# Two blocks of a transformer on one core: the modulation products of conv_ffn's out stage move into fox attention and the even mixer

## The chip, the cores and the metric

The kernel runs on one core of a Trainium2 chip. Five engines work beside each other, each through its own list of instructions: TensorE (PE, matrix products), VectorE (DVE), ScalarE (ACT), GpSimd (POOL) and SyncE (SP), which here issues nearly all DMA transfers. The metric is the device time of one execution in microseconds (us). Three runs of the kernel before took 1831.75, 1835.52 and 1836.30 us; their median is 1835.52.

## The reference

All matrices are f32, d = 1024, 256 positions (272 with 16 `meta` positions in the first block). The first block is a recurrent mixer, `conv_ffn`, forgetting attention ("fox") and `conv_ffn` again, with layer norms; the second has two layers of `swiglu`, a mixer (even: latent plus sparse attention; odd: dilated plus block attention) and `swiglu`. Every part of the second block is modulated by columns that depend on the input `c` alone:

```python
def conv_ffn(x, w_in, conv_w, conv_b, w_out):
    h = causal_dwconv(x @ w_in, conv_w, conv_b)
    gate, val = h[..., :D_FF], h[..., D_FF:]
    return (jax.nn.gelu(gate) * val) @ w_out

def modulate(x, g, shift, scale):
    return rms_norm(x, g) * (1.0 + scale[:, None, :]) + shift[:, None, :]

def swiglu(y, w_in, w_out):
    a, b = jnp.split(y @ w_in, 2, axis=-1)
    return (jax.nn.silu(a) * b) @ w_out
```

Shift, scale and gate of the six modulated parts are `silu(c) @ ada_w + ada_b`, for each layer a vector of 9216 numbers out of a 1024 x 9216 matrix. They need nothing of the activations, so their products may be computed at any time before their part begins.

## The kernel before, in words

Activations lie transposed, channels on the 128 partitions and positions along the row. Each f32 product is three matmuls (`mm3`, lines 54 to 56) of operands split into a high and a low part: ACT casts the high part of a weight block `raw` to `wh` (line 47), DVE subtracts it to get `wl` (line 50, POOL in a few places). Weights come by 1 MB DMAs that SP issues in the order of the program into five buffers `raw`; `wh` and `wl` have five buffers each as well. A DMA waits on SP for its buffer, and whatever SP issues afterwards waits behind it.

The stages follow each other: recurrent mixer, conv_ffn(0) to about 390 us, fox to about 550, conv_ffn(1) to about 770, swiglu(0,0) to about 967, even mixer to about 1115, swiglu(0,1) and swiglu(1,0) to about 1510, odd mixer to about 1635, swiglu(1,1).

*The modulation* (`ada`, line 859 and after) is cut into 72 units. A unit brings one megabyte of `ada_w` into a `raw` buffer (line 869), beside the weights, and multiplies its four blocks of 128 x 512 by a column of `silu(c)` each and adds them up on DVE: line 878 opens a sum, line 880 adds to it, so an even unit is one of 878 and three of 880, an odd unit four of 880. After every second unit the sum's columns are formed: four small matmuls (line 890) over the partitions, a copy on ACT (line 894), a transpose on PE (line 896), an addition on DVE (line 899). `ada_late` puts these some units behind. `self.plan` says in which step of which stage a unit stands: "conv" for the steps of conv_ffn's first product, "out" for the steps of the second product (`gemm_out`), for conv_ffn and swiglu alike, "swiglu" for the steps of swiglu's first product. `scales`, which needs the columns of a part, issues what is still missing.

*conv_ffn's first product* goes in steps of 128 channels: PE fills a PSUM tile `pg`, ACT (584) and DVE (586) add up the three shifted copies, ACT (607) and POOL (608) form gate times value, ACT (47) and POOL (50) split it. *Fox* begins with projections: ACT and DVE compute the forget gates' sums (lines 690 to 718, `atanh_series` at 547 to 551), PE transposes the values, DVE copies them to `V` and `vM` (lines 645, 646), and PE's line 654 multiplies `vM`, ahead of the scores (798 to 802). Its attention is run by `pipeline`, which calls `fill` between the jobs. *Modulated parts* begin with sums of squares on PE (966), POOL (992), a reciprocal root on DVE (341 to 343) and the product with x (973, 976, 980, 983).

The order on each engine is made by a scheduler: it simulates the program with costs of its own and puts instructions that need nothing of each other in another order than they are written in. Products of `ada`, which need only their weights, are often pulled ahead by it.

Of the kernel before, what the change touches and what calls it, by code (L numbers as in the profile page):

```python
# [26 lines left out]
class Kernel:  # L27
# [93 lines left out]
    def gemm_out(self, W, K, xs, epilogue, load=None, mid=None, before=None, pool=False):  # L121
# [3 lines left out]
        for half in range(2):  # L125
# [3 lines left out]
            for k0, kn in groups:  # L129
# [28 lines left out]
                if not last and k0:  # L158
                    self.ada(int(K > 2000 and (half, k0) in self.plan["out"]))
# [465 lines left out]
    def fox(self):  # L625
# [50 lines left out]
        for g in range(2):  # L676
# [55 lines left out]
            if g == 0:  # L732
                steps = (
                    self.gemm_steps(W, [(512, 512)], self.xh, self.xl, 0, L, k_epi),
                    self.gemm_steps(Wq, [(512, 512)], self.xh, self.xl, 14, L, q_epi),
                )
                self.pipeline(jobs, lambda i: 0 <= i < 8 and next(steps[i // 4], None))
# [3 lines left out]
        def fill(i):  # L741
            if i >= 0:
                next(first, None)
                next(sg, None)
            if i > 2:
                gate(3 + i // 2)
# [112 lines left out]
    def ada(self, n):  # L859
# [4 lines left out]
        for _ in range(min(n, 72 - self.ada_i)):  # L864
# [7 lines left out]
            if k0 == 0:  # L872
                self.ada_sum = self.tile([128, 512], "p")
# [11 lines left out]
    def ada_sums(self, l, b, s):  # L885

        nc = self.nc
        ps = self.psum("s")
        for j in range(4):
            nc.tensor.matmul(  # L890
                ps[32 * j : 32 * j + 32, 0:128], self.onesD[:, 0:32], s[:, j * 128 : j * 128 + 128], start=True, stop=True
            )
        e = self.tile([128, 128], "e")
        nc.scalar.activation(e, ps[:, 0:128], AF.Copy, scale=float(D))

        def columns():
            ps = self.psum("s")
            self.transpose(ps[:, 0:128], e)
            nc.vector.tensor_add(
                self.mod[l][:, 4 * b : 4 * b + 4],  # L900
                ps[:, 0:128].rearrange("p (j r) -> p j r", r=32)[:, :, 0],
                self.col_ada[l][:, 4 * b : 4 * b + 4],
            )

        self.late.append((self.ada_i + 1, 18 * l + b, columns))
# [104 lines left out]
    def swiglu(self, l, f):  # L1010
# [49 lines left out]
        for c0 in range(0, DF2, 256):  # L1060
# [40 lines left out]
            self.ada(int(c0 // 256 in self.plan["swiglu"]))  # L1101
# [123 lines left out]
    def even_mixer(self, l):  # L1225
# [23 lines left out]
        for cs in ((1440, 280), (928, 512)):  # L1249
            for _ in steps(*cs):  # L1250
                if i == 4:
# [32 lines left out]
        def fill(i):  # L1284
# [9 lines left out]
            if i > 2:  # L1294
                next(side, None)

# [695 lines left out]
    def run(self, upto=99):  # L1992
        tc, a = self.tc, self.a
        with (
# [5 lines left out]
            bufs = {"raw": 5, "wh": 5, "wl": 5, "e": 9, "p": 5, "pt": 3, "st": 8, "G": 4, "ns": 7, "st0": 1, "st1": 4, "st4": 3, "st5": 3}  # L2000
            pb = {"g": 4, "s": 4}

            def tile_(shape, tag, dt=F32, bufs_=None, **kw):
# [9 lines left out]
                "swiglu": range(9),  # L2013
# [124 lines left out]
```

## Time and profile before

| | |
|---|---|
| median of three runs | 1835.52 us |
| the profiled execution | 1832.26 us |
| its span | 1830.5 us |
| PE busy, share of the span | 1771.1 us, 97% |
| DVE busy | 1390.4 us, 76% |
| ACT busy | 1013.3 us, 55% |
| POOL busy | 427.3 us, 23% |
| HBM read | 358.21 MB, 196 GB/s |

The profile is of one execution. PE's busy time includes matmuls at half clock, so a stretch at half clock costs time without an idle row. A row of a timeline gives start, duration, engine, line, operation, tiles, how many instructions are merged in it, and in brackets how long the engine idled ahead of it and what released it.

### The profile page before, as it was taken

To read this page: it belongs to the slowest core of one execution; us is meant where nothing else is said; L and a number is where in the kernel's file an instruction comes from. 1 tells how busy PE (TensorE), PEld (TensorE's weight loads), DVE (VectorE), ACT (ScalarE), POOL (GpSimd) and SP (SyncE) were. 2 spreads that over 40 slices of the span, in tenths; PEclk is the share of its full clock that TensorE was granted. 3 is DMA by queue.
4 is the path that set the end of the run, shared out by engine and by line. 5 is a ranking of instruction groups with operands and counts; after the bars stand their busy time and mean duration, and the time that the engine had idled before them with its cause. 6 is when DMAs were issued, how large, how long until landed. Compare 5 with 4: busy or idle time off the path is not lost.

```text
span 1830.5 us, 34951 instructions
## 1 busy us (share of the span) xinstructions
PE 1771.1 (97%) x13819; PEld 1672.7 (91%) x13819; DVE 1390.4 (76%) x2500; ACT 1013.3 (55%) x1803; POOL 427.3 (23%) x430
## 2 busy tenths in 40 slices
PE   9999999999998999989999899999999999999999
PEld 8998999998888989889998659999999999889998
DVE  7989987887679787898666868877786668866543
ACT  6965765465557554454436656544454436565442
POOL 0025332230245332432101302211022110013210
PEclk9999999999999999999999999999999999999999
DMA  7553667744344767569774704988597874536550
GB/s 210 154 185 114 221 224 242 247 151 143 113 133 149 241 210 253 185 209 322 248 243 159 197 13 157 335 268 295 194 297 244 286 249 139 173 93 201 177 199 30
DMA packets 290564, 361.55 MB, mean 198 GB/s; under 512 B 12464, under 2 KB 208687, under 8 KB 290400
## 3 DMA queue, kind: packets, MB, share of 16 engines
q1 hardware_dynamic: 290096, 359.14, 60.3%
q8 instruction: 109, 1.79, 0.4%
q14 instruction: 55, 0.45, 0.1%
q10 hardware_dynamic: 304, 0.18, 0.0%
HBM read 358.21 MB, written 1.08 MB: 196 GB/s over the span
## 4 chain that ended last, share of the span: by engine, by line
PE 77%; DVE 10%; ACT 3%; issue 2%; POOL 1%; DMA 0%; DVEq 0%; POOLq 0%; ACTq 0%
PE pg L54 22%; PE pg L56 21%; PE pg L55 21%; DVE wl L50 2%; PE pg L1129 2%; PE pg L1127 2%; PE pg L1128 2%; PE ps L186 1%; PE ps L1199 1%; DVE e L586 1%; DVE B L311 1%; ACT wh L47 1%; PE ps L890 1%; DVE p L880 0%; POOL e L608 0%
## 5 line engine op out<-in xcount | busy, mean ns | idle before, releaser
L47 ACT CAST wh<-raw 128x1024 fp32r<-128x1024 f32 (+5 forms) x553 | 547.3, 998 | 515.3 <-PE pg L55 364.7
L50 DVE TENSOR_TENSOR wl<-raw,wh 128x1024 fp32r<-128x1024 f32 (+5 forms) x547 | 644.4, 1185 | 233.9 <-ACT wh L47 232.0
L54 PE MATMUL pg<-B,wh 128*128 128x256 f32 (+4 forms) x2136 | 622.2, 292 | 6.1 <-DVE e L586 4.1
L56 PE MATMUL pg<-B,wl 128*128 128x256 f32 (+4 forms) x2136 | 608.9, 285 | 2.2 <-DVE wl L50 2.2
L55 PE MATMUL pg<-B,wh 128*128 128x256 f32 (+5 forms) x2104 | 598.3, 284 | 4.3 <-POOL B L983 2.5
L55 PE MATMUL pg<-xl,wh 128*128 128x256 f32 (+4 forms) x1688 | 480.3, 285 | 0.5 <-POOL xl L983 0.5
L54 PE MATMUL pg<-xh,wh 128*128 128x256 f32 (+4 forms) x1584 | 453.4, 287 | 9.4 <-DVE e L116 4.3
L56 PE MATMUL pg<-xh,wl 128*128 128x256 f32 (+4 forms) x1584 | 450.9, 285 | 2.5 <-DVE wl L50 2.5
L54 PEld LDWEIGHTS pg<-B,wh 128*128 128x128 f32 x2136 | 405.0, 190 | 23.8 <-issue 11.4
L56 PEld LDWEIGHTS pg<-B,wl 128*128 128x128 f32 x2136 | 403.8, 189 | 2.9 <-DVE wl L50 2.4
L55 PEld LDWEIGHTS pg<-B,wh 128*128 128x128 f32 (+1 forms) x2104 | 399.5, 190 | 6.7 <-POOL B L983 3.3
L55 PEld LDWEIGHTS pg<-xl,wh 128*128 128x128 f32 x1688 | 320.8, 190 | 1.1 <-POOL xl L983 0.9
L54 PEld LDWEIGHTS pg<-xh,wh 128*128 128x128 f32 x1584 | 299.7, 189 | 14.3 <-ACT wh L47 5.7
L56 PEld LDWEIGHTS pg<-xh,wl 128*128 128x128 f32 x1584 | 300.3, 190 | 3.4 <-DVE wl L50 2.9
L50 POOL TENSOR_TENSOR B<-e,B 128x256 fp32r<-128x256 f32 (+2 forms) x123 | 142.8, 1162 | 398.4 <-ACT B L47 398.4
L880 DVE SCALAR_TENSOR_TENSOR p<-raw,cact,p 128x512 f32<-128x512 f32 x252 | 201.7, 801 | 24.3 <-DMA raw<-in_ada_w 21.3
L47 ACT CAST B<-e 128x256 fp32r<-128x256 f32 (+2 forms) x147 | 60.1, 409 | 116.2 <-POOL e L608 59.7
L608 POOL TENSOR_TENSOR e<-e,e 128x272 f32<-128x272 f32 (+1 forms) x44 | 53.6, 1218 | 143.3 <-DVE e L586 58.9
L992 POOL TENSOR_TENSOR e<-e,e 128x256 f32<-128x256 f32 x30 | 29.1, 968 | 205.9 <-ACT e L988 173.3
L1127 PE MATMUL pg<-wh,xh 128*128 128x384 f32 (+3 forms) x192 | 68.0, 354 | 2.3 <-ACT xh L976 2.3
L1129 PE MATMUL pg<-wh,xl 128*128 128x384 f32 (+3 forms) x192 | 65.8, 346 | 1.2 <-DVE xl L983 1.2
L1128 PE MATMUL pg<-wl,xh 128*128 128x384 f32 (+3 forms) x192 | 66.4, 346 | 0.0
(492 smaller groups left out, 2119.8 us busy)
## 6 DMA issues: line engine op xcount, KB each, us to landing
raw<-in_ffn_w_in SPq DMA_DIRECT2D x80, 1024.0 KB
raw<-in_ada_w SPq DMA_DIRECT2D x72, 1024.0 KB
raw<-in_f_w_in SPq DMA_DIRECT2D x44, 1024.0 KB
raw<-in_ffn_w_out SPq DMA_DIRECT2D x40, 1024.0 KB
raw<-in_f_w_out SPq DMA_DIRECT2D x20, 1024.0 KB
raw<-in_a_w_in SPq DMA_DIRECT2D x11, 1024.0 KB
raw<-in_kv_w SPq DMA_DIRECT2D x8, 1024.0 KB
raw<-in_b_w_in SPq DMA_DIRECT2D x8, 1024.0 KB
```

The lines of the kernel that those rows point to most:

```text
L47: nc.scalar.copy(hi, src)
L50: (nc.vector if lo_eng == "dve" else nc.gpsimd).tensor_sub(lo, src, hi)
L54: mm(ps, wh, xh, start=start, stop=False)
L55: mm(ps, wh, xl, start=False, stop=False)
L56: mm(ps, wl, xh, start=False, stop=stop)
L186: self.nc.tensor.transpose(dst, src, self.ident[:p, :p])
L608: nc.gpsimd.tensor_mul(y, y, v)
L880: nc.vector.scalar_tensor_tensor(s, t[:, k, :], c, s, op0=OP.mult, op1=OP.add)
L992: self.nc.gpsimd.tensor_add(self.sq[0], self.sq[0], q)
L1127: nc.tensor.matmul(ps[tt], xh[:, k, ts_], hi[:, j, :], start=st, stop=False)
L1128: nc.tensor.matmul(ps[tt], xh[:, k, ts_], lo[:, j, :], start=False, stop=False)
L1129: nc.tensor.matmul(ps[tt], xl[:, k, ts_], hi[:, j, :], start=False, stop=sp)
```

## The change

The plan is written anew. conv_ffn's out stage has its own entry of three steps instead of seven; fox gets an entry of three, used twice: in the first group of pairs (`project`) and in the second (`fill`). The even mixer gets three units in its first steps and a call that forms the sums that are due in its attention. swiglu's nine units go from steps 0 to 8 to steps 2 to 9, step 5 with two. The sums of products lie in a pool of their own, `as`, of three buffers, where they shared `p` with others; their matmuls and transposes on PE keep the place that the program gives them; and a smaller scratch region for DMAs makes room for the three buffers.

```diff
--- before.py
+++ after.py
@@ -156,7 +156,7 @@
                     self.split(hi[:rows2, kn - 1, :], lo[:rows2, kn - 1, :], rawt[:rows2, q + kn - 1, :])
                 last = k0 + kn == nk
                 if not last and k0:
-                    self.ada(int(K > 2000 and (half, k0) in self.plan["out"]))
+                    self.ada(int((half, k0) in self.plan[{DF1: "convout", DF2: "out"}.get(K, "none")]))
                 if half == 1 and k0 == 2:
                     if mid:
                         mid()
@@ -734,7 +734,13 @@
                     self.gemm_steps(W, [(512, 512)], self.xh, self.xl, 0, L, k_epi),
                     self.gemm_steps(Wq, [(512, 512)], self.xh, self.xl, 14, L, q_epi),
                 )
-                self.pipeline(jobs, lambda i: 0 <= i < 8 and next(steps[i // 4], None))
+
+                def project(i):
+                    if 0 <= i < 8:
+                        next(steps[i // 4], None)
+                    self.ada(int(i in self.plan["fox"]))
+
+                self.pipeline(jobs, project)
         first = self.fox_first(qT, kT, vM, cc, selL, maskL, O)
         sg = self.gemm_steps(Wq, [(1024, 512), (1536, 512)], self.xh, self.xl, 14, L, sg_epi)
 
@@ -742,6 +748,7 @@
             if i >= 0:
                 next(first, None)
                 next(sg, None)
+            self.ada(int(i in self.plan["fox"]))
             if i > 2:
                 gate(3 + i // 2)
 
@@ -870,7 +877,7 @@
                 t, a["ada_w_2"][l, k0 * 128 : (k0 + 4) * 128, b * 512 : b * 512 + 512].rearrange("(k p) c -> p k c", p=128)
             )
             if k0 == 0:
-                self.ada_sum = self.tile([128, 512], "p")
+                self.ada_sum = self.tile([128, 512], "as")
             s = self.ada_sum
             for k in range(4):
                 c = self.cact[:, k0 + k : k0 + k + 1]
@@ -886,16 +893,19 @@
 
         nc = self.nc
         ps = self.psum("s")
+        keep = self.tc.keep_in_program_order
         for j in range(4):
-            nc.tensor.matmul(
-                ps[32 * j : 32 * j + 32, 0:128], self.onesD[:, 0:32], s[:, j * 128 : j * 128 + 128], start=True, stop=True
+            keep(
+                nc.tensor.matmul(
+                    ps[32 * j : 32 * j + 32, 0:128], self.onesD[:, 0:32], s[:, j * 128 : j * 128 + 128], start=True, stop=True
+                )
             )
         e = self.tile([128, 128], "e")
         nc.scalar.activation(e, ps[:, 0:128], AF.Copy, scale=float(D))
 
         def columns():
             ps = self.psum("s")
-            self.transpose(ps[:, 0:128], e)
+            keep(nc.tensor.transpose(ps[:, 0:128], e, self.ident))
             nc.vector.tensor_add(
                 self.mod[l][:, 4 * b : 4 * b + 4],
                 ps[:, 0:128].rearrange("p (j r) -> p j r", r=32)[:, :, 0],
@@ -1098,7 +1108,7 @@
                 nc.vector.tensor_mul(y[:jw], y[:jw], pb_)
                 hi, lo = gs(k)
                 self.split(hi, lo, y[:jw], lo_eng="pool")
-            self.ada(int(c0 // 256 in self.plan["swiglu"]))
+            self.ada(self.plan["swiglu"].count(c0 // 256))
         self.warm(y[:jw])
         self.gemm_out(a["ffn_w_out_2"][l, f], DF2, gs, self.residual(gate, {(0, 0): True, (0, 1): (1, 0), (1, 0): True}.get((l, f))))
 
@@ -1248,6 +1258,7 @@
         i = 0
         for cs in ((1440, 280), (928, 512)):
             for _ in steps(*cs):
+                self.ada(int(i in (0, 1, 2)))
                 if i == 4:
                     ch, tab = self.mla_low(j, z, st)
                 if i == 5:
@@ -1293,6 +1304,8 @@
                 squares()
             if i > 2:
                 next(side, None)
+            if i == 9:
+                self.ada_late(36)
 
         self.pipeline(mla + nsa, fill)
         Wo = a["ev_w_out_2"][j]
@@ -1997,7 +2010,7 @@
             tc.tile_pool(name="dram", bufs=1, space=DRAM) as self.dp,
         ):
             orig = self.tile
-            bufs = {"raw": 5, "wh": 5, "wl": 5, "e": 9, "p": 5, "pt": 3, "st": 8, "G": 4, "ns": 7, "st0": 1, "st1": 4, "st4": 3, "st5": 3}
+            bufs = {"raw": 5, "wh": 5, "wl": 5, "e": 9, "p": 5, "pt": 3, "st": 8, "G": 4, "ns": 7, "as": 3, "st0": 1, "st1": 4, "st4": 3, "st5": 3}
             pb = {"g": 4, "s": 4}
 
             def tile_(shape, tag, dt=F32, bufs_=None, **kw):
@@ -2010,7 +2023,10 @@
             self.n = 0
             self.plan = {
                 "conv": (3, 5, 7, 9),
-                "swiglu": range(9),
+                "swiglu": (2, 3, 4, 5, 5, 6, 7, 8, 9),
+                "convout": ((0, 8), (1, 4), (1, 12)),
+                "fox": (0, 3, 6),
+                "none": (),
                 "out": ((0, 4), (0, 8), (0, 12), (1, 4), (1, 8), (1, 12), (1, 16)),
             }
 
@@ -2124,7 +2140,7 @@
     import concourse.bacc as bacc
     from concourse.bass_utils import run_bass_kernel_spmd
 
-    nc = bacc.Bacc("TRN2", target_bir_lowering=False, num_devices=1)
+    nc = bacc.Bacc("TRN2", target_bir_lowering=False, num_devices=1, dynamic_dma_scratch_size=512)
     arrays = {f"in_{n}": np.ascontiguousarray(inputs[n]) for n in _INS}
     arrays.update({f"in_{n}": v for n, v in constants().items()})
     args = {
```

The scheduler makes an order of its own of this. DVE at the beginning of fox, before: line 547 opens the series for the forget gates, `m_668` is its running value, and lines 645 and 646, behind these rows, copy the values for line 654 of PE.

```order
L547 TENSOR_TENSOR m_667_4757<-e_4750 16x272
L548 TENSOR_SCALAR m_668_4758<-m_667_4757 16x272
L550 SCALAR_TENSOR_TENSOR m_668_4758<-m_668_4758,m_667_4757 16x272 x2
L50 TENSOR_TENSOR wl_5035<-raw_4995,wh_5034 128x1024
L550 SCALAR_TENSOR_TENSOR m_668_4758<-m_668_4758,m_667_4757 16x272 x4
L50 TENSOR_TENSOR wl_5098<-raw_5095,wh_5097 128x1024
L551 SCALAR_TENSOR_TENSOR m_668_4758<-m_668_4758,e_4750 16x272
```

The same place in the changed program, whose lines after `ada` stand seven further down: 885 and 887 are what 878 and 880 were, `as` the sums.

```order
L547 TENSOR_TENSOR m_655_4711<-e_4704 16x272
L887 SCALAR_TENSOR_TENSOR as_4303<-raw_5088,cact_1541,as_4303 128x512
L548 TENSOR_SCALAR m_656_4712<-m_655_4711 16x272
L887 SCALAR_TENSOR_TENSOR as_4303<-raw_5088,cact_1541,as_4303 128x512
L550 SCALAR_TENSOR_TENSOR m_656_4712<-m_656_4712,m_655_4711 16x272
L50 TENSOR_TENSOR wl_4989<-raw_4949,wh_4988 128x1024
L550 SCALAR_TENSOR_TENSOR m_656_4712<-m_656_4712,m_655_4711 16x272
L885 TENSOR_SCALAR as_5249<-raw_5247,cact_1541 128x512
L550 SCALAR_TENSOR_TENSOR m_656_4712<-m_656_4712,m_655_4711 16x272
L50 TENSOR_TENSOR wl_5052<-raw_5049,wh_5051 128x1024
L550 SCALAR_TENSOR_TENSOR m_656_4712<-m_656_4712,m_655_4711 16x272
L887 SCALAR_TENSOR_TENSOR as_5249<-raw_5247,cact_1541,as_5249 128x512
```

Four products stand between the series' operations here. From line 714 to the last copy of line 646 there are eight, seven of 887 and one of 885; a ninth stands ahead of line 714.

DVE at the end of conv_ffn(1), before; `pg` are PE's results, and the last line 586 of the stage stands twelve rows behind these, with a product of line 880 ahead of it.

```order
L586 SCALAR_TENSOR_TENSOR e_8157<-pg_8132,col_f1a_1519,e_8157 128x256
L878 TENSOR_SCALAR p_8431<-raw_8429,cact_1541 128x512
L586 SCALAR_TENSOR_TENSOR e_8157<-pg_8132,col_f1a_1519,e_8157 128x256
L880 SCALAR_TENSOR_TENSOR p_8431<-raw_8429,cact_1541,p_8431 128x512
L50 TENSOR_TENSOR wl_8359<-raw_8356,wh_8358 128x1024
L586 SCALAR_TENSOR_TENSOR e_8190<-pg_8165,col_f1a_1519,e_8190 128x256
L880 SCALAR_TENSOR_TENSOR p_8431<-raw_8429,cact_1541,p_8431 128x512
L586 SCALAR_TENSOR_TENSOR e_8190<-pg_8165,col_f1a_1519,e_8190 128x256
L880 SCALAR_TENSOR_TENSOR p_8431<-raw_8429,cact_1541,p_8431 128x512
L586 SCALAR_TENSOR_TENSOR e_8227<-pg_8202,col_f1a_1519,e_8227 128x256
```

The same end in the changed program; the last two lines 586 stand ten rows behind these.

```order
L586 SCALAR_TENSOR_TENSOR e_8129<-pg_8104,col_f1a_1519,e_8129 128x256
L887 SCALAR_TENSOR_TENSOR as_8142<-raw_8443,cact_1541,as_8142 128x512
L586 SCALAR_TENSOR_TENSOR e_8129<-pg_8104,col_f1a_1519,e_8129 128x256
L887 SCALAR_TENSOR_TENSOR as_8142<-raw_8443,cact_1541,as_8142 128x512
L50 TENSOR_TENSOR wl_8352<-raw_8321,wh_8351 128x1024
L586 SCALAR_TENSOR_TENSOR e_8180<-pg_8155,col_f1a_1519,e_8180 128x256
L887 SCALAR_TENSOR_TENSOR as_8142<-raw_8443,cact_1541,as_8142 128x512
L586 SCALAR_TENSOR_TENSOR e_8180<-pg_8155,col_f1a_1519,e_8180 128x256
L50 TENSOR_TENSOR wl_8382<-raw_8379,wh_8381 128x1024
L586 SCALAR_TENSOR_TENSOR e_8213<-pg_8188,col_f1a_1519,e_8213 128x256
L887 SCALAR_TENSOR_TENSOR as_8142<-raw_8443,cact_1541,as_8142 128x512
L586 SCALAR_TENSOR_TENSOR e_8213<-pg_8188,col_f1a_1519,e_8213 128x256
```

The second half of a sum stands here one step earlier than the first half did before, and no product behind it up to the stage's end.

DVE at the beginning of the even mixer, before: lines 341 to 343 are the reciprocal root, 973 the first product with `x`.

```order
L341 SCALAR_TENSOR_TENSOR e_11522<-ps_11506,m_1627_11521 128x256
L342 SCALAR_TENSOR_TENSOR e_11522<-e_11522,m_1627_11521 128x256
L343 SCALAR_TENSOR_TENSOR m_1627_11521<-e_11522,m_1627_11521 128x256
L973 TENSOR_TENSOR p_11527<-x_72,m_1627_11521 128x512
L973 TENSOR_TENSOR p_11535<-x_72,m_1627_11521 128x512
```

The same place in the changed program; line 983 is what 973 was.

```order
L887 SCALAR_TENSOR_TENSOR as_11649<-raw_11677,cact_1541,as_11649 128x512
L885 TENSOR_SCALAR as_11704<-raw_11702,cact_1541 128x512
L341 SCALAR_TENSOR_TENSOR e_11499<-ps_11483,m_1621_11498 128x256
L887 SCALAR_TENSOR_TENSOR as_11649<-raw_11677,cact_1541,as_11649 128x512
L342 SCALAR_TENSOR_TENSOR e_11499<-e_11499,m_1621_11498 128x256
L887 SCALAR_TENSOR_TENSOR as_11649<-raw_11677,cact_1541,as_11649 128x512
L343 SCALAR_TENSOR_TENSOR m_1621_11498<-e_11499,m_1621_11498 128x256
L887 SCALAR_TENSOR_TENSOR as_11704<-raw_11702,cact_1541,as_11704 128x512
L983 TENSOR_TENSOR p_11504<-x_72,m_1621_11498 128x512
L983 TENSOR_TENSOR p_11512<-x_72,m_1621_11498 128x512
```

Five products of the units of the mixer's first steps stand around the reciprocal root: two ahead of line 341 and three between it and the product with `x`.

## Rows read from the trace of the kernel before

**Rows 1.** the page: span, and busy time with share and instructions of each engine

```profile
span 1830.5 us, 34951 instructions
...
PE 1771.1 (97%) x13819; PEld 1672.7 (91%) x13819; DVE 1390.4 (76%) x2500; ACT 1013.3 (55%) x1803; POOL 427.3 (23%) x430
```

**Rows 2.** PE's longest waits: who waits for whom, us in total, times, longest

```profile
PE pg L54 <- DVE e L586: 5.7, 3, 2.3
PE pg L56 <- DVE wl L50: 4.6, 3, 2.2
```

**Rows 3.** the page: line, form, count, busy us, mean ns, idle before and releaser

```profile
L880 DVE SCALAR_TENSOR_TENSOR p<-raw,cact,p 128x512 f32<-128x512 f32 x252 | 201.7, 801 | 24.3 <-DMA raw<-in_ada_w 21.3
```

**Rows 4.** windows: length; PE, PEld, DVE, ACT, POOL busy; clock, DMA share, GB/s

```profile
270.00:370.00 100.00, 99.38 (x806) 97.50 (x805) 79.54 (x108) 49.40 (x73) 24.95 (x24) 1.00 0.75 249
396.00:428.00 32.00, 30.21 (x236) 28.22 (x235) 28.20 (x61) 16.52 (x32) 0.61 (x2) 1.00 0.65 206
676.00:692.00 16.00, 11.76 (x82) 11.04 (x81) 14.36 (x31) 7.31 (x14) 5.69 (x5) 0.79 0.78 276
768.00:800.00 32.00, 22.93 (x161) 20.50 (x161) 31.12 (x54) 19.21 (x35) 20.04 (x19) 0.95 0.34 103
966.00:976.00 10.00, 8.26 (x50) 7.07 (x50) 7.95 (x19) 6.02 (x13) 1.34 (x2) 1.00 0.17 52
1026.00:1064.00 38.00, 31.45 (x218) 22.83 (x208) 30.87 (x141) 23.73 (x71) 11.93 (x8) 0.82 0.64 167
```

**Rows 5.** PE in order of time, 418 to 426 us: start, us, operation, idle before

```profile
422.58 1.04 PE L654 MATMUL ps<-B,m 16*64 16x512 f32 x2 [1.79 <-issue]
```

**Rows 6.** PE in order of time, end of conv_ffn(1)

```profile
684.41 0.36 PE L54 MATMUL pg<-B,wh 128*128 128x256 f32 x1 [2.29 <-DVE e L586]
...
687.14 0.55 PE L54 MATMUL pg<-B,wh 128*128 128x256 f32 x1 [1.78 <-DVE e L586]
```

**Rows 7.** PE in order of time, first steps of swiglu(0,0)

```profile
772.78 1.72 PE L966 MATMUL ps<-e,onesD 128*128 128x256 f32 x6 [3.12 <-POOL e L992]
...
791.80 0.39 PE L55 MATMUL pg<-B,wh 128*128 128x256 f32 x1 [1.24 <-POOL B L983]
...
799.35 0.39 PE L56 MATMUL pg<-B,wl 128*128 128x256 f32 x1 [2.17 <-DVE wl L50]
```

**Rows 8.** DVE in order of time, end of conv_ffn(1)

```profile
680.15 0.48 DVE L878 TENSOR_SCALAR p<-raw,cact 128x512 f32<-128x512 f32 x1
680.55 0.48 DVE L586 SCALAR_TENSOR_TENSOR e<-pg,col_f1a,e 128x256 f32<-128x256 f32 x1
680.94 0.74 DVE L880 SCALAR_TENSOR_TENSOR p<-raw,cact,p 128x512 f32<-128x512 f32 x1
681.60 1.22 DVE L50 TENSOR_TENSOR wl<-raw,wh 128x1024 fp32r<-128x1024 f32 x1
```

**Rows 9.** DVE in order of time, beginning of fox

```profile
400.69 0.18 DVE L714 CAST eh<-m 128x16 fp32r<-128x16 f32 x1 [1.67 <-DMA m<-in_const_fox]
...
422.22 0.27 DVE L646 COPY B<-ps 16x128 f32<-16x128 f32 x1
```

**Rows 10.** line 880 alone: what its engine waited for, us and times

```profile
  DMA raw<-in_ada_w: 21.3, 11
```

**Rows 11.** SyncE's DMA issues in order of time, beginning of fox

```profile
394.88 0.37 SPq L67 DMA_DIRECT2D raw<-in_kv_w  x1
```

**Rows 12.** DVE in order of time, first steps of swiglu(0,0)

```profile
788.48 0.75 DVE L880 SCALAR_TENSOR_TENSOR p<-raw,cact,p 128x512 f32<-128x512 f32 x1
...
789.93 1.23 DVE L880 SCALAR_TENSOR_TENSOR p<-raw,cact,p 128x512 f32<-128x512 f32 x1
```

**Rows 13.** POOL in order of time, the same steps

```profile
789.76 0.85 POOL L1042 TENSOR_TENSOR e<-e,m 128x256 f32<-128x256 f32 x1 [2.01 <-DVE e L1041]
```

**Rows 14.** DVE in order of time, beginning of the even mixer

```profile
969.63 0.42 DVE L341 SCALAR_TENSOR_TENSOR e<-ps,m 128x256 f32<-128x256 f32 x1 [1.27 <-ACT m L340]
```

**Rows 15.** PE in order of time, beginning of the even mixer

```profile
972.38 0.46 PE L1127 MATMUL pg<-wh,xh 128*128 128x416 f32 x1 [1.14 <-ACT xh L976]
```

## The prediction

> **What bounds the kernel now.** I read the page's first part first: TensorE (PE) is busy for 1771.1 us of a span of 1830.5 [rows 1], so only the 59.4 us in which it idles, and the stretches at half clock, can be won or enlarged. The second view is the list of PE's waits [rows 2]: the matmuls behind DVE's line 586 lost 5.7 us in three waits and those behind DVE's `wl` 4.6 in three. Nearly all of it lies at the ends and beginnings of stages. The third view is the page's table of costly groups [rows 3]: the products that this change moves are 252 VectorE (DVE) operations of line 880, 201.7 us in all, and DVE stood idle ahead of them for 21.3 us until their weights had landed. They hold up PE only where DVE is already late. So I looked at windows around the places to which, and from which, they go [rows 4]: in 396 to 428 us DVE is busy for 28.20 of 32 us, in 768 to 800 for 31.12, while POOL works for 0.61 us in the first and 20.04 in the second. The reader is to see there that the beginning of fox is as full for DVE as a border is.
>
> The window's clock gives a price for lost speed. [...]
>
> **What the change adds and removes.** The order of the programs has the same products, sums and transfers; they only stand elsewhere. The price of one moved product is its start-to-start distance on DVE where it does not meet POOL: line 880 starts at 680.94 and the next operation at 681.60, so 0.66 us; line 878, which opens a sum, starts at 680.15 and its follower at 680.55, so 0.40 [rows 8].
>
> *Beginning of fox.* PE stops at line 654 until DVE has copied the last piece of `vM`: DVE's last line 646 starts at 422.22 and lasts 0.27, PE goes on at 422.58 after 1.79 us [rows 5, 9]. From 400.69 to 422.49 DVE's operations follow each other without a hole. The new order puts into just this chain, between line 714 and the last copy, seven products of line 880 and one of 878: 7 x 0.66 + 0.40 = 5.0 us. A ninth stands ahead of line 714, where DVE idles 1.67 us for `const_fox` [rows 9]; it costs nothing if its weights are there. In PE's order one matmul more than before stands ahead of line 654, so nothing covers the 5.0 us, and the wait becomes 6.8. A wait that long has no row; the nearest, 3.12, was followed by 1.6 us of lost clock, and I add that: +6.6. Lower end: another 1.67 us of DVE's idle time absorbs products and the clock stays, 5.0 - 1.67 = +3.3. Upper end: DVE stops at a product whose weights are late. On average such a stop took 1.9 us (21.3 over 11 stops, [rows 10]); with 3.4 of clock that is 5.0 + 1.9 + 3.4 = +10.3. The transfers speak for some of that: the new order has a megabyte of `ada_w` in the place of the `kv_w` that is issued at 394.88, ahead of `const_fox` [rows 11], and that `kv_w` goes behind the masks, with a second `ada_w` directly behind it. Whatever `wl` of it is late on DVE stands in the same chain and is not counted twice.
>
> *End of conv_ffn(1).* PE waits 2.29 and 1.78 us there for line 586 [rows 6], because DVE takes two half units of products in its last nine steps. The new order has one, and nothing behind the third step from the end. I take it that the 2.29 us go and a wait like the 1.78 stays, and with it half of the 3.4 us of clock: -4.0. Nothing at all if the four products, which now stand one step earlier, make the same two waits; -(2.29 + 1.78 + 3.4) = -7.5 if both go.
>
> Here the trace also shows what POOL does to the price. At 788.48, with POOL idle, line 880 lasts 0.75 us; at 789.93, beside POOL's line 1042, which runs from 789.76 to 790.61, 1.23 [rows 12, 13]. [...]
>
> *swiglu(0,0), first steps.* The products of steps 0 and 1 leave. PE's waits of 1.24 (for POOL) and 2.17 (for `wl`, which stood behind a product) can go: -3.4 [rows 7]. But the unit of step 2 is pulled ahead into the normalisation, with three products between its operations: 3 x 0.66 = +2.0. I take -1.4; ends -3.4 and +2.0.
>
> *Beginning of the even mixer.* A new load: three units at its first steps. Two products stand ahead of line 341, where DVE idles 1.27 us [rows 14]; 0.66 + 0.40 fit into it. Three more stand between lines 341, 342, 343 and the first product with `x`, in the chain for whose result, by way of ACT's `xh`, PE waits already 1.14 us [rows 15]. So +2.0, without cover. Ends: 0 if ACT's part hides it; 2.0 + 1.9 + 1.6 = +5.5 if one megabyte is late and the clock falls. The DMA engines are only 0.17 busy in that window [rows 4], which speaks for weights in time.
>
> *Other places.* At the beginnings of swiglu(0,1) and swiglu(1,0) one product each now stands between lines 341 and 343, and others that stood behind are gone: 2 x 0.66 = +1.3, ends -1 and +2.6 (four products). In conv_ffn(0)'s out stage four units go away, but PE is busy there for 99.38 of 100 us [rows 4], so 0. In the middle of the even mixer the order of many small operations changes, and a column sum of the moved units comes in; 0.18 x 38 = 6.8 us are lost to the clock in that window [rows 4], and I cannot tell a direction: 0, ends -5 and +5. Pinning the sums' matmuls and their own pool remove no wait that the list shows: 0, within the ends of the even mixer.
>
> **Sum.** 6.6 - 4.0 - 1.4 + 2.0 + 1.3 = +4.5 us. The profiled execution took 1832.26 us, 1.76 around its span; the median of the runs is 1835.52, 3.3 above it. On the profiled one the sum gives 1836.8, on the median 1840.0, which is what I predict. A difference below 0.3% (5.5 us) cannot be told from none in this kernel; the forecast is slightly slower within that.
>
> **Rivals.**
> *The new products' weights are late* (the slower side). The place is fox's line 654 and the even mixer's border; the price is their upper ends: 10.3 - 4.0 - 1.4 + 5.5 + 1.3 = +11.7, 1847.2 us. For it: DVE takes its work in order, and has 21.3 us of such stops already. Against: 16 DMA engines are only 0.65 and 0.17 busy in the two windows [rows 4]. It decides when a product's transfer lands after the operation ahead of it on DVE has ended.
>
> *The old waits go wholly, and the new ones are short* (the faster side). Both waits at the end of conv_ffn(1) go with the clock's 3.4, both at swiglu's, fox pays only 3.3: 3.3 - 7.5 - 3.4 = -7.6, 1827.9 us. For it: the loop there is carried from step to step, so that a lag once avoided also avoids the next; where POOL works, products were dear. Against: four products still stand in the last five steps. It decides when the granted clock stays at 1.00 from 676 to 692.
>
> *Everything is hidden.* If the copies of `vM` came earlier in DVE's order than I read, or PE had other work there, fox would cost nothing and the rest come to -4.0 - 1.4 + 2.0 + 1.3 = -2.1, 1833.4 us. PE's order ahead of line 654 speaks against it.
>
> **Chances and range.** Forecast, 1834 to 1845: 0.48 (of it 0.31 within 0.3%, 0.17 above). Late weights: 0.23 (0.21 slower). Old waits gone wholly: 0.20 (0.17 faster). Hidden: 0.09 (0.06 within, 0.03 faster). So faster 0.20, same 0.42 (0.05 from the outer cases), slower 0.38. The range is 1827 to 1851: the faster rival's value, and the slower one's 1847.2 with the gain at conv_ffn(1) gone, 4.0. The even mixer's 5 us to either side remain partly outside. The likeliest's own range is 1834 to 1845.
>
> **What would show it.** Right: at fox's line 654 a wait of PE of 6 to 9 us behind DVE's line 646, and products of line 880 between lines 550 and 646; at the end of conv_ffn(1) one wait above 1 us instead of two, clock above 0.79; ahead of the even mixer's first matmul a wait near 3 us instead of 1.14. Wrong: a wait at line 654 below 3 us (then the time is about 1833), or the even mixer's middle moving by more than 5 us, which no term here carries.

## The result

The changed kernel took 1848.12 us (median of five runs, 1843.02 to 1850.20) against 1835.52 of the kernel before (five runs as well): a ratio of 1.0070, 95% interval 1.0059 to 1.0082. It is slower by 12.6 us, inside the range of 1827 to 1851, but on the far side of the 0.3% within which the forecast of 1840 lay. The profiled execution took 1850.2 us, the upper end; that of the kernel before took 1832.26, near its lower end. The two spans below therefore differ by 17.9 us, five more than the medians, and figures by stage add up to the 17.9.

The page after, span and busy time, beside [rows 1]:

```profile
span 1848.4 us, 34967 instructions
...
PE 1779.7 (96%) x13819; PEld 1681.7 (91%) x13819; DVE 1388.1 (75%) x2500; ACT 1013.8 (55%) x1803; POOL 438.9 (24%) x430
```

PE's busy time grew by 8.6 us although it has the same 13819 matmuls: for the most part they ran at half clock for longer. The mean granted clock over the span is 0.983 where it was 0.989, and 0.006 x 1848 = 11 us, idle time included. Its idle time grew from 59.4 to 68.7 us. PE's waits in the changed kernel (who waits for whom, us in total, times, longest):

```profile
PE ps L976 <- POOL e L1002: 7.9, 5, 4.1
PE ps L654 <- issue: 5.9, 1, 5.9
...
PE pg L1137 <- ACT xh L986: 3.5, 2, 2.3
...
PE pg L54 <- DVE e L586: 3.1, 3, 1.9
...
PE pg L54 <- DVE e L1060: 2.5, 1, 2.5
PE pg L56 <- DVE wl L50: 2.5, 2, 1.7
```

The two waits of [rows 2] shrank, 5.7 to 3.1 and 4.6 to 2.5; line 654 rose from 1.8 to 5.9, and waits at the beginnings of modulated parts are new or longer (line 976's were 6.2 us in total and 3.1 at the longest). To see where the time went I laid the two traces beside each other by their product matmuls, which are the same 4088 in the same order but for a few neighbours: the table gives by how many us a stretch between two of them is longer than in the kernel before. (*Whole* is the changed kernel, the others are experiments below; profiles of one execution each, so a single figure below 2 us says little.)

| stretch, us in the kernel before | whole | no products at fox's start | even units late | plan only | plan, no even units | pool only | swiglu(0,0) steps only |
|---|---|---|---|---|---|---|---|
| fox's beginning, 392 to 428 | +7.6 | +3.1 | +7.7 | +4.7 | +4.8 | +0.1 | -0.1 |
| fox, 428 to 535 | +2.7 | +6.2 | +2.8 | +3.2 | +3.2 | 0.0 | 0.0 |
| end of conv_ffn(1)'s first product, 676 to 704 | -1.4 | -2.5 | -3.1 | -2.7 | -3.0 | -0.3 | -0.5 |
| swiglu(0,0), beginning, 745 to 812 | -2.4 | -2.4 | -2.4 | -3.9 | -3.8 | +2.8 | -4.0 |
| even mixer, beginning, 960 to 992 | +8.1 | +6.6 | +8.1 | +6.6 | +0.5 | 0.0 | 0.0 |
| even mixer, middle, 992 to 1087 | -3.4 | -2.2 | -2.4 | +3.8 | -1.1 | +2.8 | -0.4 |
| swiglu(0,1), beginning, 1110 to 1142 | +2.7 | +3.4 | +4.8 | +2.7 | 0.0 | +2.4 | 0.0 |
| swiglu(1,1), 1655 to 1822 | +1.9 | +1.9 | 0.0 | +1.9 | 0.0 | +1.9 | +1.9 |

The last stretch has no products and the same work in all of them; its 1.9 us come and go with the execution, and the kernel before's profile is one without them.

Not all of a difference is a loss: small matmuls of the sums, and others of the mixer, stand in another stretch than before. Fox holds 19 more (860 in place of 841). The even mixer's beginning holds 27 more (219 in place of 192), of which 18 come from its middle, so these two rows are to be read as one, +4.7. Of the +8.1, 2.9 are idle time of PE (4.77 against 1.84) and about 1.7 half clock (0.83 over 975 to 985 us).

*Fox's beginning.* DVE in order of time, beside [rows 9] (885 and 887 are what 878 and 880 were):

```profile
399.18 0.75 DVE L887 SCALAR_TENSOR_TENSOR as<-raw,cact,as 128x512 f32<-128x512 f32 x1 [0.96 <-DMA raw<-in_ada_w]
399.84 0.17 DVE L714 CAST eh<-m 128x16 fp32r<-128x16 f32 x1
...
405.96 0.73 DVE L887 SCALAR_TENSOR_TENSOR as<-raw,cact,as 128x512 f32<-128x512 f32 x1
406.63 0.28 DVE L548 TENSOR_SCALAR m<-m 16x272 f32<-16x272 f32 x1
...
422.64 1.52 DVE L887 SCALAR_TENSOR_TENSOR as<-raw,cact,as 128x512 f32<-128x512 f32 x2
...
425.55 0.27 DVE L646 COPY B<-ps 16x128 f32<-16x128 f32 x1
```

From the start of line 714 to the start of the last line 646 it takes 25.71 us; before it took 21.53 (400.69 to 422.22). The eight products lengthen it by 4.18 us, a little less than their 5.0, since some fill short gaps between operations that need each other (from line 547 to line 548 it was 0.46 us; with a product between them it is 0.35 + 0.67). PE waits for it, beside [rows 5], and its clock falls; the second fence is the window of 422 to 432 us (columns as in [rows 4]):

```profile
425.92 1.93 PE L654 MATMUL ps<-B,m 16*64 16x512 f32 x2 [5.88 <-issue]
```

```profile
422.00:432.00 10.00, 6.08 (x26) 3.15 (x26) 8.46 (x22) 1.55 (x4) 0.00 (x0) 0.52 0.80 242
```

5.88 - 1.79 = 4.1 us are the wait, and most of the rest of 7.6 is the clock, which is 0.52 here; in windows of 2 us it is 0.50 from 424 to 432 us, the half clock. The same window in the kernel before:

```profile
422.00:432.00 10.00, 9.41 (x71) 7.77 (x72) 7.93 (x33) 6.15 (x18) 0.42 (x2) 1.00 0.63 201
```

*The end of conv_ffn(1).* PE in order of time, beside [rows 6]; these are its only waits there:

```profile
692.92 0.36 PE L54 MATMUL pg<-B,wh 128*128 128x256 f32 x1 [0.61 <-DVE e L586]
694.97 0.36 PE L54 MATMUL pg<-B,wh 128*128 128x256 f32 x1 [1.10 <-DVE xh L959]
698.33 0.55 PE L54 MATMUL pg<-B,wh 128*128 128x256 f32 x1 [0.59 <-DVE e L586]
```

In place of 2.29 + 1.78 = 4.07 us it waits 2.30, but the clock is 0.79 over 16 us (686 to 702) once more.

*The even mixer's beginning.* DVE and PE in order of time, beside [rows 14, 15]; line 983 is the first product with x, 993 what 983 was:

```profile
978.51 0.42 DVE L341 SCALAR_TENSOR_TENSOR e<-ps,m 128x256 f32<-128x256 f32 x1 [1.81 <-ACT m L340]
978.85 0.74 DVE L887 SCALAR_TENSOR_TENSOR as<-raw,cact,as 128x512 f32<-128x512 f32 x1
...
985.23 0.74 DVE L887 SCALAR_TENSOR_TENSOR as<-raw,cact,as 128x512 f32<-128x512 f32 x1
...
987.21 0.75 DVE L887 SCALAR_TENSOR_TENSOR as<-raw,cact,as 128x512 f32<-128x512 f32 x1
```

```profile
975.09 2.79 PE L976 MATMUL ps<-e,onesD 128*128 128x256 f32 x6 [0.73 <-POOL e L1002]
982.88 0.45 PE L1137 MATMUL pg<-wh,xh 128*128 128x416 f32 x1 [2.32 <-ACT xh L986]
...
990.99 0.45 PE L1139 MATMUL pg<-wh,xl 128*128 128x416 f32 x1 [1.31 <-POOL xl L993]
```

The wait for ACT's `xh` doubles (1.14 to 2.32). Two further products, which I had not read in the order, stand between DVE's operations for POOL, and PE waits 1.31 us for that; and the matmuls of line 976 run at half clock (0.50 from 976 to 978 us; 2.79 us for six, 1.13 for four before). Ahead of all this DVE stands 1.55 us, until 970.84, for a megabyte of `ada_w`, by the order of the units the one that SP issued at 965.63, after a wait of 5.9; behind that product comes line 1012, whose `x` goes by way of ACT and POOL to line 976.

### The profile page after: what moved, and what is told of

It is laid out like the page before. It is cut to its first block, busy times and chain, and to the rows that moved or that the text cites. A ratio compares the mean times of both kernels' runs of the same rounds, so it can differ in the third digit from the quotient of the medians.

```text
span 1848.4 us, 34967 instructions
## 1 busy us (share of the span) xinstructions
PE 1779.7 (96%) x13819; PEld 1681.7 (91%) x13819; DVE 1388.1 (75%) x2500; ACT 1013.8 (55%) x1803; POOL 438.9 (24%) x430
## 3 DMA queue, kind: packets, MB, share of 16 engines
q8 instruction: 109, 1.79, 0.4%
## 4 chain that ended last, share of the span: by engine, by line
PE 71%; DVE 11%; ACT 4%; issue 3%; POOL 3%; DMA 1%; DVEq 0%; POOLq 0%; ACTq 0%
PE pg L54 20%; PE pg L55 19%; PE pg L56 19%; DVE wl L50 3%; PE pg L1139 1%; DVE e L586 1%; PE pg L1137 1%; PE pg L1138 1%; ACT wh L47 1%; POOL e L608 1%; DMA raw<-in_ada_w 1%; PE ps L186 1%; DVE as L887 1%; PE ps L1209 1%; DVE B L311 1%
## 5 line engine op out<-in xcount | busy, mean ns | idle before, releaser
L50 POOL TENSOR_TENSOR B<-e,B 128x256 fp32r<-128x256 f32 (+2 forms) x123 | 148.8, 1210 | 397.2 <-ACT B L47 397.2
L887 DVE SCALAR_TENSOR_TENSOR as<-raw,cact,as 128x512 f32<-128x512 f32 x252 | 202.4, 803 | 34.6 <-DMA raw<-in_ada_w 31.4
```

The source lines that it names most:

```text
L50: (nc.vector if lo_eng == "dve" else nc.gpsimd).tensor_sub(lo, src, hi)
L887: nc.vector.scalar_tensor_tensor(s, t[:, k, :], c, s, op0=OP.mult, op1=OP.add)
```

## The experiments

Each was timed against the kernel before on the same chip; the ratio stands with its interval. In the first one `ada(..., True)` leaves products out; in the two after it it holds the unit's products on DVE behind what the program issues there before them.

**Fox: the transfers without most of the products.**

```diff
-            for k in range(4):
+            for k in range(1 if hold else 4):
...
-                    self.ada(int(i in self.plan["fox"]))
+                    self.ada(int(i in self.plan["fox"]), True)
```

> The changed kernel, but of each of fox's first three units only one of the four products is formed (the other nine are left out, so the modulation columns of that unit are incomplete); their three 1 MB transfers stand in the same places of SyncE's order. Theory A (the products stand in VectorE's chain ahead of the copies that PE's line 654 waits for): the wait at line 654 falls from 5.88 us to 2 to 3 us, the half clock behind it goes, and the time falls by 5 to 7 us against the changed kernel, to about 1842. Theory B (the transfers take weight buffers and come ahead of const_fox and kv_w): the wait stays at 5 us or more and the time near 1848.

1845.49 us, 1.0070 (1.0055 to 1.0085). The experiment leaves out nine of the twelve products of these units. The wait only fell to 4.72 us:

```profile
423.57 1.93 PE L654 MATMUL ps<-B,m 16*64 16x512 f32 x2 [4.72 <-issue]
```

Theory A was wrong about this kernel, and theory B too, in its reason: DVE stood in the chain for a product's weights.

```profile
406.91 0.49 DVE L885 TENSOR_SCALAR as<-raw,cact 128x512 f32<-128x512 f32 x1 [1.83 <-DMA raw<-in_ada_w]
```

1.83 us of waiting, 0.40 for this product and 0.66 for the next make 2.9, and 1.79 + 2.9 = 4.7. So DVE's chain is what PE waits for in both kernels; with nine products less, DVE arrives earlier at one whose megabyte has not landed, and saves little. What costs is a product in the chain, by its own time or by its weights'.

**Fox: nothing at its beginning.**

```diff
-                    self.ada(int(i in self.plan["fox"]))
...
-            self.ada(int(i in self.plan["fox"]))
+            self.ada(int(i in (0, 1, 3, 4, 6, 7)), True)
```

> The changed kernel with fox's six units all in the second group of pairs, their products held on VectorE behind what is written before them: neither products nor transfers at fox's beginning. Theory A and B alike: wait at line 654 back to about 1.8 us and clock 1.00 there; 7.4 us less than the changed kernel, about 1841. If six units in the second group cost PE something, it shows between 470 and 550 us as a loss of more than 1.9 us (that of the changed kernel), and the time is above 1842.

1844.30 us, 1.0058 (1.0043 to 1.0073). The wait at line 654 came back to 1.75 us, as both theories had it, but the clock did not:

```profile
421.32 1.66 PE L654 MATMUL ps<-B,m 16*64 16x512 f32 x2 [1.75 <-issue]
```

```profile
422.00:432.00 10.00, 10.00 (x56) 7.87 (x55) 5.63 (x20) 4.78 (x13) 0.42 (x2) 0.68 0.50 156
```

0.32 x 10 = 3.2 us of work lost behind a wait of 1.75, where 1.79 before lost nothing. And six units in the second group lengthen it by 6.2 us in place of 2.7: 2.4 of these are idle time of PE, 1.7 half clock, and the rest mostly the sums' own 27 matmuls. Fox does not hide the units.

**The even mixer: units later, products held.**

```diff
-                self.ada(int(i in (0, 1, 2)))
+                self.ada(int(i in (1, 2, 3)), True)
```

> The changed kernel with the even mixer's three units one step later and their products held on VectorE behind what is written before them, so that none stands between lines 341 and the last xl of the modulation. Theory A (products in the root's chain and among the xl products): the 5.1 us lost there (7.2 to 12.3 us behind the kernel before) shrink to 0 to 1.5, the time falls by 4 us to about 1844. Theory C (the loss comes from half clock behind a wait of POOL on line 1002, not from the products): 2 us or more of the loss stay.

1848.78 us, 1.0087 (1.0071 to 1.0102): no gain. The border itself was cured; PE's wait for `xh` is 1.15 us again, the 1.31 for POOL is gone. But the loss came back 15 us later, as weights that ACT waits for, 1.97 us, and then PE. SP's transfers in the kernel before, and in this one, and ACT:

```profile
945.27 13.52 SPq L67 DMA_DIRECT2D raw<-in_ev_w_in  x4
965.08 16.76 SPq L67 DMA_DIRECT2D raw<-in_mla_w_uq  x2
```

```profile
957.94 12.94 SPq L876 DMA_DIRECT2D raw<-in_ada_w  x3
987.70 1.03 SPq L67 DMA_DIRECT2D raw<-in_ev_w_in  x2
991.08 1.03 SPq L67 DMA_DIRECT2D raw<-in_mla_w_uq  x2
```

```profile
992.88 1.05 ACT L47 CAST wh<-raw 128x1024 fp32r<-128x1024 f32 x1 [1.97 <-DMA raw<-in_ev_w_in]
```

Three megabytes of `ada_w`, issued between 958 and 971 us, lie in three of the five `raw` buffers until DVE reads them at 984 and later, and the mixer's own weights cannot be issued: `mla_w_uq`, issued from 965.08 before, goes out from 991.08. From 975 to 985 us the DMA engines are 0.00 busy. In the changed kernel the same three transfers go out from 959.72; DVE reads them earlier, inside the chain. Either way it is paid.

**Only the sums' part.**

```diff
-                self.ada_sum = self.tile([128, 512], "p")
+                self.ada_sum = self.tile([128, 512], "as")
...
+            keep(nc.tensor.transpose(ps[:, 0:128], e, self.ident))
```

> The kernel before with only the sums' part of the change: their matmuls and transposes held in PE's order, their own pool of three buffers, the smaller DMA scratch; the plan is the old one. Theory A: within 0.15% of the kernel before (1833 to 1838), since no wait on the sums was seen. Rival D: the held order itself costs PE time, 3 to 6 us, where a sum is not ready at its place.

1843.20 us, 1.0060 (1.0042 to 1.0079), with the plan of before. Theory A, and the prediction's zero for this part, were wrong; two more runs divide it.

**The plan without the sums' part.**

```diff
-                self.ada_sum = self.tile([128, 512], "as")
+                self.ada_sum = self.tile([128, 512], "p")
...
-            keep(
-                nc.tensor.matmul(
+            nc.tensor.matmul(
...
-    nc = bacc.Bacc("TRN2", target_bir_lowering=False, num_devices=1, dynamic_dma_scratch_size=512)
+    nc = bacc.Bacc("TRN2", target_bir_lowering=False, num_devices=1)
```

> The changed kernel without the sums' part: sums in the shared pool p, their matmuls free to move, the DMA scratch of before; the new plan stays. Theory E (plan and sums' part add up: the sums' part costs about 10 us by itself, the plan the rest): about 3 to 6 us above the kernel before, 1837 to 1840, with a wait of 4 to 6 us at line 654. Theory A (the plan is all of it): 12 us above, about 1846.

1848.76 us, 1.0087 (1.0068 to 1.0106). The two parts do not add up: the plan alone is as slow as the whole.

**The pool alone, and the holding alone.** The first edit is the pool's, with the smaller scratch, the second the holding's, each in the kernel before.

```diff
-                self.ada_sum = self.tile([128, 512], "p")
+                self.ada_sum = self.tile([128, 512], "as")
```

```diff
-            self.transpose(ps[:, 0:128], e)
+            keep(nc.tensor.transpose(ps[:, 0:128], e, self.ident))
```

> The kernel before with the sums' own pool of three buffers and the smaller DMA scratch; nothing held, the plan is the old one. Theory F (three buffers of their own let or make the scheduler place products elsewhere, and that is the 10 us): 6 to 10 us above the kernel before, with a wait of 3 us or more ahead of swiglu(0,0) for line 258. Theory G (holding the sums' matmuls and transposes in PE's order does it): within 2 us of the kernel before.

> The kernel before with the sums' matmuls and transposes held in PE's order, in the shared pool p and with the scratch of before. Theory G: 6 to 10 us above the kernel before. Theory F: within 2 us of it.

The pool with the smaller scratch: 1841.11 us, 1.0042 (1.0026 to 1.0059). The holding: 1833.40, 1.0004 (0.9993 to 1.0016), nothing. So it is the pool (or the scratch that makes room for it), and what differs is the order: with it 150 of DVE's 2500 instructions stand elsewhere than before, with the holding five. One place of it, DVE ahead of swiglu(0,0), and PE behind it:

```profile
754.36 1.54 DVE L880 SCALAR_TENSOR_TENSOR as<-raw,cact,as 128x512 f32<-128x512 f32 x2 [3.36 <-DMA raw<-in_ada_w]
755.81 0.75 DVE L258 TENSOR_TENSOR B<-B,pg 128x256 f32<-128x256 f32 x2
```

```profile
756.61 1.22 PE L290 MATMUL ps<-B,onesD 128*128 128x256 f32 x2 [3.31 <-DVE B L258]
```

Two products were put ahead of line 258, and the first stands there 3.36 us for its weights; PE waits 3.31 behind them, where it waited 0.83 before. Why the scheduler put them there I have not shown. Pool and scratch were not tried apart.

**Fewer units at the end of conv_ffn's first product.**

```diff
-                    self.ada(int(K > 2000 and (half, k0) in self.plan["out"]))
+                    self.ada(int((half, k0) in self.plan[{DF1: "convout", DF2: "out"}.get(K, "none")]))
...
+                "convout": ((0, 12), (1, 4), (1, 8), (1, 12), (1, 16)),
...
+            self.ada(int(i in (2, 5)))
```

> The kernel before with conv_ffn's out stage at five units, without the first two steps' ones whose products are pulled into the end of the first product, two units in fox's second group of pairs, no other part of the change. From the stages of the changed kernel: 1.4 to 2.5 us less at the end of conv_ffn(1), nothing at fox's beginning: 1831 to 1834, if fox's second group hides two units; 1836 to 1838 if they cost there what six cost in the kernel with none at its beginning (3.5 us).

1838.01 us, 1.0031 (1.0021 to 1.0040): the second case. Two units in fox's second group cost 2.6 us there, and only 0.8 was gained at conv_ffn(1).

**The plan without the even mixer's units.**

```diff
-                self.ada(int(i in (0, 1, 2)))
...
-            if i == 9:
-                self.ada_late(36)
```

> The new plan alone (sums in p, nothing held) without the even mixer's three units and its call for the sums. Theory H (the three units cost the even mixer what the table of stages shows, by products in the root's chain and by holding three of the five weight buffers): even_begin and even_mid come back from +10.4 us to within 2 of the kernel before; the time falls to 1836 to 1840. Rival (the new order of the even mixer's small operations loses it, units or not): 4 us or more stay and the time is above 1841.

1840.05 us, 1.0034 (1.0021 to 1.0047), 8.7 us below the plan with them (on another chip; by the ratios 0.5%); the mixer's two stretches fell from +10.4 to -0.6. So it is the units that cost it, as theory H has it; how much of it products in the chain and how much occupied buffers, this run does not divide. A new loss, 7.6 us in swiglu(0,1), hides part of it: PE stood 4.42 us at a sum's transpose. Is holding the sums the cure for that?

> The new plan without the even mixer's units, and the sums' matmuls and transposes held in PE's order (in the shared pool p). In the same kernel without the holding PE stood 4.42 us at a sum's transpose that waited for ACT's copy, and 1.41 us more ahead of a score matmul behind another copy. Theory: the holding was the cure for these, and under the new plan it gains 5 to 7.6 us (the stage sw01 from +7.6 to 0 to 2): 1833 to 1836. Rival (the transposes wait as long where they are held): within 2 us of the 1840 without it.

1840.77 us, 1.0038 (1.0026 to 1.0050): the rival; what makes the loss in swiglu(0,1) stays open. The held transpose waits as long:

```profile
1249.22 0.48 PE L908 MATMUL ps<-con,e 128*128 128x128 f32 x1 [4.62 <-ACT e L904]
```

**One piece alone: swiglu(0,0)'s steps; and with it three units from conv_ffn(1).**

```diff
-            self.ada(int(c0 // 256 in self.plan["swiglu"]))
+            self.ada(((2, 3, 4, 5, 5, 6, 7, 8, 9) if (l, f) == (0, 0) else self.plan["swiglu"]).count(c0 // 256))
```

> The kernel before with one piece of the change alone: in swiglu(0,0), and there only, the nine units in steps 2 to 9 instead of 0 to 8. Theory: the 2.4 to 3.9 us that its first steps gained in the changed kernels come without the losses elsewhere: 1828 to 1830, ratio 0.998. Rival (the order moves elsewhere too and takes it back, as it did with the sums' pool): within 1 us of the kernel before.

> The same, and the first three units of conv_ffn(1)'s out stage go to swiglu(0,0) as well (twelve units in steps 2 to 9), so that no product stands in the last nine steps of conv_ffn(1)'s first product. Theory: both waits of 2.29 and 1.78 us there go and with them the half clock (together up to 7.5 us), and swiglu(0,0)'s 2.4 to 3.9: 1822 to 1827. Rival (PE waits there for its own loop of DVE, POOL and ACT, the products only add to it): a gain of 2 to 3 us there, about 1828.

The first: 1830.27 us, 0.9973 (0.9962 to 0.9984), faster than both kernels, with 4.0 us gained in swiglu(0,0)'s first steps and nothing lost elsewhere. PE there, beside [rows 7]:

```profile
781.25 0.39 PE L55 MATMUL pg<-B,wh 128*128 128x256 f32 x1 [1.72 <-DVE B L983]
786.39 0.39 PE L55 MATMUL pg<-B,wh 128*128 128x256 f32 x1 [1.00 <-POOL B L983]
789.79 0.38 PE L55 MATMUL pg<-B,wh 128*128 128x256 f32 x1 [0.56 <-POOL B L983]
```

The 2.17 us for `wl` at 799.35 are gone. The second: 1830.39 us, 0.9982 (0.9973 to 0.9992), its rival's case by the gain, though 2.4 us above the rival's time. No product stands at conv_ffn(1)'s end any more, and yet PE waits once for 2.72 us, now behind the casts of line 949:

```profile
682.91 0.55 PE L54 MATMUL pg<-B,wh 128*128 128x256 f32 x1 [2.72 <-DVE xh L949]
```

It gains 2.8 us there and gives most of it back in swiglu(0,0), which has three units more.

## Why the prediction was right, and where it was wrong

The likeliest case gave +4.5 us, "slightly slower within" 0.3%; measured were +12.6, outside the likeliest case's own 1834 to 1845. The direction and the wide range held, the size did not. That the wide range held is in part luck: its upper end was priced with late weights at fox, and what filled it were costs elsewhere that the sum had at nothing or too low. Of the signs of being right, products stand in fox's chain, with a wait of 5.88 us where 6 to 9 were said; one wait above 1 us is left at the end of conv_ffn(1), but the clock is not above 0.79; ahead of the even mixer's first matmul PE waits 2.32 us instead of nearly 3.

- *Fox's beginning*, +6.6 forecast, +7.6 measured. The step was right in place and mechanism. The wait grew by 4.1 instead of 5.0, because the eight products lengthened the chain by 4.18 us only, and the clock took more than the 1.6 assumed, about 3. The 1.6 and 3.4 us for the clock in the sum and its ends are what two windows of [rows 4] lost, 0.05 x 32 and 0.21 x 16; that a new wait brings the same loss again was an estimate that no run shows as a rule. Measured were about 3 here, and 0.21 x 16 = 3.4 again at the end of conv_ffn(1), from 686 to 702 us. The experiment with nothing at fox's beginning shows that this clock price is not tied to the long wait alone.
- *Rest of fox*, cost at nothing by silence, +2.7 measured: 1.7 are half clock without an idle of PE before it (0.72 over 496 to 502 us), and about 1 is the work of 19 matmuls of the sums that stood elsewhere before. The kernels with two and six units in the second group have 2.6 and 6.2 more there.
- *End of conv_ffn(1)*, -4.0 forecast, -1.4 measured, -2.5 to -3.5 in kernels with the same plan. The old waits went, and three shorter ones, 2.30 us together, stand where one of 1.78 was expected; that the clock would recover half was wrong here, it is 0.79 over 16 us again. The upper end of -7.5 was not reached without any product either: a wait of 2.72 stays.
- *swiglu(0,0)*, -1.4 forecast, -2.4 measured and -4.0 alone. The gain of -3.4 was sized about right: in the kernel with these steps alone, and in that with the plan alone (-3.9), no product stands between lines 341 and 343. In the changed kernel, with the sums' pool, three do, as forecast; the 1.5 us between -2.4 and -3.9 fit the 2.0 charged for them, which no run shows by itself.
- *Even mixer*, +2.0 forecast, +4.7 over both its stretches, and taking the units out of the plan gives 11 back there. This is the step that failed in kind. The three products were in the root's chain, but PE's wait for `xh` grew by 1.2 us only; 1.31 for POOL, behind two products that I did not read because I stopped at the first product with `x`, five rows before, and 1.7 of half clock, behind a wait of 0.73 at line 976, were at nothing in the sum. "The DMA engines are only 0.17 busy in that window [rows 4], which speaks for weights in time" looked at the wrong resource: a transfer waits for one of five buffers, of which the units take three (where their products are held, `mla_w_uq` goes out from 991.08 us, before from 965.08). So a megabyte of `ada_w` came 1.55 us late ahead of line 1012, as the rival with late weights has it; that the wait and half clock at line 976 come of this is not shown. Where the products are held out of the chain, the mixer's own weights are late instead (1.97 us).
- *Other borders*, +1.3 forecast, +2.7 at swiglu(0,1)'s beginning, nothing at swiglu(1,0)'s. One product was counted at each; in the trace three stand about line 341 of swiglu(0,1), two of them behind line 1048, which ends DVE's idle time, so that all three count, and PE waits 2.5 us for line 1060.
- *The sums' part*, 0 forecast. Held sums: right, 1.0004. Their own pool, with the smaller scratch: wrong, 8 us by itself. I had looked for waits that it would remove and not for what the new order does at places that the plan does not touch. In the whole change it does not add to the plan's loss; the plan alone is 1.0087, the whole 1.0070, and the intervals overlap.

Of the rivals, "the new products' weights are late" with 1847.2 came nearest in time, but its own mechanism is not what the trace shows at fox: there the only stop for weights, 0.96 us, stands ahead of line 714, where the forecast had room for it. Over the whole kernel DVE's stops for `ada_w` did grow, from 21.3 us in 11 to 31.4 in 17 at line 880 (at line 878 they fell from 16.9 to 13.6); how much of that PE feels is not shown.

## What to carry to other kernels

Work that "may be done at any time" was bought here with three things at the place where it went: time on its engine in front of whatever waits there (4.18 us of DVE's chain at fox), a buffer from the moment its transfer is issued until it is read (from 958 to 984 us in the even mixer with the products held), and the order of everything that a scheduler places around it (150 of DVE's 2500 instructions with the pool). Look at all three where the work arrives, not only at the waits where it leaves. Time the pieces of a change by themselves: here one of them, a few steps of one stage, was worth 4 us alone, while the whole cost 12.6; and the pieces did not add up.

## What the runs showed of the hardware

The half clock followed the length of PE's wait only in part. All fourteen traces of this case have the wait at line 654. Six of them have 3.37 to 6.16 us there, and half clock came with each: behind 5.88, 4.72 and 3.43 us (the changed kernel, fox with the transfers only, the plan alone) the clock is 0.52, 0.54 and 0.69 from 422 to 432 us. Eight have 1.65 to 2.23, and it came with one: behind 1.75 in the kernel with nothing at fox's beginning the clock was 0.68 over 10 us, while 1.79 in the kernel before and 2.23 in the one with fewer units at conv_ffn's end left the clock at 1.00. Elsewhere in the changed kernel it began behind a wait of 0.73 (line 976; 0.50 from 976 to 978 us), and between 484 and 500 us it fell to 0.92 without any idle of PE:

```profile
484.00:500.00 16.00, 16.00 (x133) 14.39 (x133) 12.99 (x54) 9.44 (x29) 8.12 (x27) 0.92 0.37 114
```

What decides the cost of a short wait is not shown: 1.75 and 1.79 us, next to each other in length, had 0.68 and 1.00 behind them. For a forecast from these traces, a term of about 3 us behind a wait of about 2 us at this line is a chance and not a sum: one of the eight paid it, 3.2 us. Behind the waits of 3.37 and more it was paid every time.
